# FFN gate and up: hi and lo parts of x as one 512-column moving operand, accumulator halves added afterwards, and new start addresses for TensorE's operands

## The chip, the cores and the metric

One core of a Trainium2 chip runs the whole program. The metric is the device time of one execution in microseconds (us), as a median of several runs. TensorE is called PE in the rows, its weight loads PEld, VectorE DVE, ScalarE ACT, GpSimd POOL, SyncE SP.

## What is computed

A trunk of two layers over 256 tokens of width 1024, all in float32. Cut to what matters here:

```python
D_MODEL = 1024; SEQ = 256; DEPTH = 2; D_FF = 2816

def swiglu(x, wg, wu, wd):
    return (jax.nn.silu(x @ wg) * (x @ wu)) @ wd

for i in range(DEPTH):
    h = h + 0.5 * swiglu(rmsnorm(h, ffn1_norm[i]), ffn1_wg[i], ffn1_wu[i], ffn1_wd[i])
    h = h + hybrid_mixer(rmsnorm(h, mix_norm[i]), ...)
    h = h + 0.5 * swiglu(rmsnorm(h, ffn2_norm[i]), ffn2_wg[i], ffn2_wu[i], ffn2_wd[i])
    gate = jax.nn.sigmoid(rmsnorm(h, ple_norm[i]) @ ple_w_gate[i])
    h = h + gate * (p[i] @ ple_w_proj[i])
return rmsnorm(h, final_norm)
```

So the FFN half-step stands four times in the program: twice in each layer.

## The kernel before

Every large product is done with both operands split into two float32r parts, hi and lo, whose sum is the float32 value. Three products are added in PSUM: hi with hi, hi with lo, lo with hi. Weights come from HBM in chunks of 1 MB, each loaded as two halves (`raw`, five slots) on SP's queue. Each half is split by `split` (lines 97 and 98): ACT copies `raw` to `whi`, DVE subtracts to get `wlo`. `whi` and `wlo` have seven slots each (`NHALF`), so that three and a half chunks are live: the half that is split when half n gives its slot back is half n + 7.

The activations of a stage are turned to [feature, token] and split into `xhi` and `xlo`, eight blocks of 128 features by 256 tokens (`xpair`). Products come in two forms. In `ws` the weights are stationary and 256 columns of x move; `ws2` does two blocks of 128 features into the two halves of one PSUM bank. In `as_` a 128 by 128 block of activations is stationary and up to 512 columns of weights move. All are emitted through `mm` (line 77), so that they share a line; the operands tell them apart, as (moving, stationary).

An FFN stage has 22 chunks of gate and up weights (128 gate features beside 128 up features). The first three go through `up_head`, per token tile and with the activations stationary. The other 19 go through `up(j)`: `ws2` over eight k blocks (48 matmuls of 256 columns) and then `evac(j)`: ACT's Silu of the gate half (line 344), DVE's product with the up half (line 346), and the split into `hh[j]` and `hl[j]`. Then `down` multiplies with `hh` and `hl` stationary, 512 columns of weights moving, for 11 chunks. The stationary activations elsewhere are `xhi`, `xlo` (among others in `Narrow`, the w_o and w_pg projections), `yh`, `yl` (the mixer's second output projection) and `ph`, `pl` (the embedding).

At a stage's seam, `closing`, `prepare` and `turn` run the norm of one token tile under the products of the other. At the very end `Last` (lines 917 to 933) multiplies h by the gain into `xn`, scales it and stores it, tile 0 first. The order on each engine is set by a scheduler of the tile framework from this program order; queues are followed in order.

In the program as built, where an operand begins in its partition, modulo 512 bytes, is: 160 for `whi`, `wlo`, `xhi` and `xlo`; 32 for `hh`, `hl`, `ph` and `pl`; 352 for `yh` and `yl`.

Of the kernel before, what the change touches and what calls it, by code (L numbers as in the profile page):

```python
# [17 lines left out]
NT = 2  # L18
# [17 lines left out]
W2 = NT * HEADS  # L36
ORDER = ("bc8 sc0.0 xs0 sc0.1 bc10 sc0.2 xs1 sc1.0 sc1.1 sc1.2 xs2 xs3 z1.0 sc2.0 sc2.1 z1.1 sc2.2 xs4 bc9 bc11 xs5 "
# [19 lines left out]
def trunk(ctx: ExitStack, tc: tile.TileContext, a: dict, out: bass.AP):  # L57
# [11 lines left out]
    def nm(s):  # L69
        cnt[0] += 1  # L70
        return f"{s}_{cnt[0]}"

    def bank():
        return psp.tile([P, 512], F32, tag="ps", name=nm("ps"))
# [4 lines left out]
    # ---- constants  # L79
# [7 lines left out]
    mhalf = cst.tile([P, 1], F32, name="mhalf")  # L87
    nc.vector.memset(mhalf, -0.5)

    # ---- weights: loaded once each, split into two float32r parts that add up to the float32  # L90
# [14 lines left out]
    def half(raw, kn):  # L105
        """Half a chunk: kn row blocks of 128 as a list of (hi, lo), each [128, CH / 2 / kn]"""
        hi = wp.tile([P, CH // 2], F32R, tag="whi", name=nm("whi"), bufs=NHALF)
        lo = wp.tile([P, CH // 2], F32R, tag="wlo", name=nm("wlo"), bufs=NHALF)
        split(hi, lo, raw)
        hv, lv = (w.rearrange("p (k c) -> p k c", k=kn) for w in (hi, lo))  # L110
        return [(hv[:, k], lv[:, k]) for k in range(kn)]

    # The program is a list of items, emitted in order at the end: (function, keys of the weight chunks it
    # reads). The loads and splits of later chunks are emitted as soon as earlier items have freed their slots.
# [5 lines left out]
    def chunk(name, i, c, kn):  # L120
        """Registers a chunk of weights of kn row blocks; its key"""
        key = (name, i, c)
        sources[key] = (a[name][i, c], kn)
        return key
# [46 lines left out]
    def xpair():  # L171
        hi = act.tile([P, KD, NT, P], F32R, tag="xhi", name=nm("xhi"), bufs=2)
        lo = act.tile([P, KD, NT, P], F32R, tag="xlo", name=nm("xlo"), bufs=2)
        return hi, lo
# [8 lines left out]
    # small products, let in one by one between the large ones  # L183
# [6 lines left out]
    # ---- out[feature, token] for 128-feature blocks: the weights are stationary  # L190
    def ws(o, wc, cols, x, t=None):
        xh, xl = x
        for k in range(KD):
            wh, wl = wc[k]
            rh = xh[:, k] if t is None else xh[:, k, t]
            rl = xl[:, k] if t is None else xl[:, k, t]
            mm(o, wh[:, cols], rh, k == 0, False)
            mm(o, wh[:, cols], rl, False, False)
            mm(o, wl[:, cols], rh, False, k == KD - 1)
            drip()  # L200

    def ws2(ps, wc, x, t=None):
        """Two 128-feature blocks into one bank, for one token tile or both"""
        for b in range(2):
            o = ps[:, b * 256:(b + 1) * 256] if t is None else ps[:, b * 256 + t * P:b * 256 + (t + 1) * P]
            ws(o, wc, slice(b * P, (b + 1) * P), x, t)

    # ---- out[token, feature]: the activations are stationary
    def as_(os, lh, ll, rh, rl, first, last):
        """os: {column block: bank}"""  # L210
        for j, o in os.items():
            sl = slice(j * o.shape[-1], (j + 1) * o.shape[-1])
            mm(o, lh, rh[:, sl], first, False)
            mm(o, lh, rl[:, sl], False, False)
        for j, o in os.items():
            sl = slice(j * o.shape[-1], (j + 1) * o.shape[-1])
            mm(o, ll, rh[:, sl], False, last)
        drip(2)
# [5 lines left out]
    def banks_of(t, sls):  # L224
        """A token tile's accumulators, by the first of their columns"""
        return {(t, sl.start): bank()[:, 0:sl.stop - sl.start] for sl in sls}
# [4 lines left out]
    # ---- [token, feature] -> [feature, token], split  # L231
# [13 lines left out]
    def rstd(parts, scale):  # L245
        v = sm.tile([P, 1], F32, tag="var", name=nm("var"))
        if len(parts) > 1:
            nc.vector.tensor_scalar(v, parts[0], parts[1], EPS, op0=ALU.add, op1=ALU.add)
            for p in parts[2:]:
                nc.vector.tensor_tensor(v, v, p, op=ALU.add)  # L250
        else:
            nc.vector.tensor_scalar(v, parts[0], scale, EPS, op0=ALU.mult, op1=ALU.add)
        r = sm.tile([P, 1], F32, tag="rstd", name=nm("rstd"))
        nc.gpsimd.tensor_tensor(r, v, mhalf, op=ALU.pow)  # L254
        return r

    class Norm:
        """The stage's input from h, per token tile: square(t, sl) the squares of columns sl, prepare(t) the rest of the norm,
        turn(t) to [feature, token]"""
# [25 lines left out]
    # ---- a stage's end and the next one's start, the first token tile ahead of the second: each tile's  # L285
    # elementwise chain runs under the other's products
    def closing(t, steps, finish, prep):
        """The last products of a token tile, one half of the columns after the other"""
        def f(*wcs):
            with ExitStack() as order:  # L290
                if t == 1 and getattr(prep, "first", False):
                    for ins in prep.turned:
                        order.enter_context(tc.issue_after(ins))
                for sl in prep.pieces[t]:
                    for (fn, _), wc in zip(steps, wcs):
                        fn(wc, [sl])
                    finish(t, sl)
                    prep.square(t, sl)
                prep.prepare(t)
        add(f, *[k for _, keys in steps for k in keys])  # L300
# [32 lines left out]
    # ---- feed-forward half-step  # L333
    class FFN:
        def __init__(self, i, gu, dn, gname, ple=None):
# [4 lines left out]

            def evac(j):
                ps = banks.pop(j)
                sg = fp.tile([P, 256], F32, tag="sg", name=nm("sg"), bufs=3)
                nc.scalar.activation(sg, ps[:, 0:256], AF.Silu)
                pr = fp.tile([P, 256], F32, tag="pr", name=nm("pr"), bufs=3)
                nc.vector.tensor_tensor(pr, sg, ps[:, 256:512], op=ALU.mult)  # L346
                hh[j] = fp.tile([P, 256], F32R, tag=f"hh{j}", name=nm("hh"))
                hl[j] = fp.tile([P, 256], F32R, tag=f"hl{j}", name=nm("hl"))
                split(hh[j], hl[j], pr)

            def up(j):
                def f(wc):
                    banks[j] = bank()
                    ws2(banks[j], wc, prep.x)
                    evac(j)
                return f, [chunk(gu, i, j, KD)]

            def up_head(j, t):
                def f(wc):
                    if t == 0:  # L360
                        banks[j] = bank()
                    xh, xl = prep.x
# [50 lines left out]
    # ---- [tokens, K] @ [K, 1024] from four chunks, the first token tile ahead at both ends  # L413
    class Narrow:
        def __init__(self, name, i, x, pieces=(HALVES, HALVES)):
            self.acc = acc = {}

            def run(c, t):
                def f(wc, sls=pieces[t]):
                    if (t, 0) not in acc:  # L420
                        acc.update(banks_of(t, pieces[t]))
                    for k in range(2):
                        kk = c * 2 + k
                        xh, xl = x()
# [6 lines left out]
    # ---- gated per-layer embedding  # L431
    class Ple:
# [16 lines left out]
        def early(self, pool):  # L449
            """Ahead of the stage, in the pool of the one before"""  # L450
# [17 lines left out]
    # ---- token mixing  # L468
    class Mixer:
        def __init__(self, i):  # L470
# [13 lines left out]
            # B and C first: chunks 8..11 of the convolved channels  # L484
# [52 lines left out]
            def z_run(g, kh, ts):  # L537
                def f(wc):
                    xh, xl = S.prep.x
# [15 lines left out]
            # [tokens, K] @ [K, 512]: a half of a projection to D, from two chunks  # L555
# [48 lines left out]
            # the large products in ORDER; the small work by how many of them it comes after its group's last  # L604
            # inner channels
# [34 lines left out]
            # gates and output projections  # L640
# [32 lines left out]
        # the mixer's inner seam, from m_w_out to w_o  # L673
# [42 lines left out]
        def conv_silu(self, ps, blk, dst):  # L716
            """dst [P, 2, 256] = silu(conv(ps) + b) for channel blocks blk, blk + 1"""
# [29 lines left out]
        # time steps: the columns of both parts of the weights are side by side, and added after the transposes;  # L747
        # softplus(x) = max(x, 0) + log1p(e), e = exp(-|x|); log1p(e) = 2 atanh(e / (2 + e))
        def dt_raw(self):
            xh, xl = self.prep.x  # L750
# [7 lines left out]
        def steps(self):  # L758
# [16 lines left out]
            negA = mp.tile([P, HEADS], F32, tag="negA", name=nm("negA"))  # L775
# [20 lines left out]
        # cumulative sums within a chunk, in both layouts, and the first chunk's total  # L796
        def sums(self):
# [11 lines left out]
            self.w0 = w0 = mp.tile([P, HEADS], F32, tag="w0", name=nm("w0"))  # L809
# [10 lines left out]
        # state-space branch, one group of heads: C B^T under the decays  # L820
# [87 lines left out]
    # ---- the whole trunk  # L908
# [5 lines left out]
    class Last(Norm):  # L914
        """The final norm in place of a next stage's input"""
# [5 lines left out]
        def square(self, t, sl):  # L921
            super().square(t, sl)
            if sl.start == 0:
                self.xn[t] = act.tile([P, D], F32, tag=("xhi", "xlo")[t], name=nm("xn"), bufs=2)
# [13 lines left out]
    class First:  # L938
        """The load of x in place of a stage before"""
# [100 lines left out]
```

## Time and profile before

| what | value |
|---|---|
| time, median of 3 runs | 1550.38 us (1548.4 to 1552.99) |
| span of the profiled execution | 1549.5 us |
| PE busy, share of the span | 1529.4 us, 99% |
| weight loads busy | 1396.5 us, 90% |
| DVE busy | 990.3 us, 64% |
| ACT busy | 826.7 us, 53% |
| DMA | 286.38 MB, mean 185 GB/s |

The profiled execution has no time listed beside its span; the span lies between the lowest and the median time of the three runs, 0.9 us under the median. Busy times of PE count each matmul with its modelled end, so neighbours overlap: what a matmul costs in a dense stream is the distance from its start to the next one's start.

### The profile page before, as it was taken

What the parts mean: (1) busy time and instruction counts of PE and PEld (TensorE: products, weight loads), DVE (VectorE), ACT (ScalarE), POOL (GpSimd) and SP (SyncE); (2) the same over time, 40 slices, a digit from 0 to 9 for tenths busy, and PEclk for the clock granted to TensorE, in tenths of its full rate; (3) what the DMA queues carried; (4) which work ended last, traced back from release to release, by engine and by line L of the source; (5) the groups of instructions that cost most, each with busy time, mean ns of one, the idle gap of its engine ahead of it and who ended that gap; (6) DMA issues with size and microseconds to landing.
All of it is one profiled execution on the core that took longest, in us unless ns stands there. A gap on an engine that the chain in (4) does not pass through costs nothing.

```text
span 1549.5 us, 25054 instructions
## 1 busy us (share of the span) xinstructions
PE 1529.4 (99%) x10072; PEld 1396.5 (90%) x10072; DVE 990.3 (64%) x1398; ACT 826.7 (53%) x1110; POOL 25.3 (2%) x41
## 2 busy tenths in 40 slices
PE   7999999999999999999999999999999999999998
PEld 7999889999988889998899988899999887999886
DVE  5555467898865565554675554688979655755545
ACT  5554365667564355543655444675666544544444
POOL 0000000000000000000000000000000000000000
PEclk9999999999999999999999999999999999999999
DMA  7556565555646656666566654665555565665552
GB/s 282 183 188 187 187 189 186 189 186 183 197 150 192 192 186 188 187 187 187 163 201 188 186 183 151 223 198 183 192 176 180 167 191 177 206 189 181 186 152 94
DMA packets 81493, 286.38 MB, mean 185 GB/s; under 512 B 10592, under 2 KB 10976, under 8 KB 81376
## 3 DMA queue, kind: packets, MB, share of 16 engines
q1 hardware_dynamic: 74016, 268.47, 55.0%
q10 hardware_dynamic: 7360, 16.31, 3.2%
q8 instruction: 79, 1.29, 0.3%
q14 instruction: 38, 0.31, 0.1%
HBM read 283.62 MB, written 1.11 MB: 184 GB/s over the span
## 4 chain that ended last, share of the span: by engine, by line
PE 96%; DVE 2%; DMA 1%; ACT 0%; issue 0%; POOL 0%; SPq 0%; POOLq 0%; ACTq 0%; DVEq 0%
PE ps L77 94%; PE ps L238 2%; DVE wlo L98 1%; DMA raw<-in_gu 1%; PE ps L509 0%; ACT whi L97 0%; DVE xn L279 0%; POOL rstd L254 0%; DVE sg L462 0%; PE ps L377 0%; DVE h L463 0%; DVE xlo L242 0%; ACT junk L272 0%; ACT sg L461 0%; DVE h L407 0%
## 5 line engine op out<-in xcount | busy, mean ns | idle before, releaser
L98 DVE TENSOR_TENSOR wlo<-raw,whi 128x1024 fp32r<-128x1024 f32 x508 | 616.7, 1223 | 412.7 <-ACT whi L97 408.4
L97 ACT ACTIVATE whi<-raw 128x1024 fp32r<-128x1024 f32 x508 | 534.2, 1058 | 460.1 <-PE ps L77 430.4
L77 PE MATMUL ps<-xhi,whi 128*128 128x256 f32 x1984 | 571.0, 288 | 0.0
L77 PE MATMUL ps<-xhi,wlo 128*128 128x256 f32 x1984 | 561.4, 283 | 0.0
L77 PE MATMUL ps<-xlo,whi 128*128 128x256 f32 x1984 | 561.3, 283 | 0.0
L77 PEld LDWEIGHTS ps<-xhi,whi 128*128 128x128 f32 x1984 | 380.7, 192 | 2.6 <-issue 1.9
L77 PEld LDWEIGHTS ps<-xlo,whi 128*128 128x128 f32 x1984 | 380.8, 192 | 2.5 <-issue 2.4
L77 PEld LDWEIGHTS ps<-xhi,wlo 128*128 128x128 f32 x1984 | 380.5, 192 | 0.0
L77 PE MATMUL ps<-whi,xhi 128*128 128x512 f32 (+1 forms) x648 | 234.9, 364 | 0.4 <-ACT whi L97 0.2
L77 PE MATMUL ps<-wlo,xhi 128*128 128x512 f32 (+1 forms) x648 | 231.8, 358 | 1.2 <-DVE wlo L98 1.2
L77 PE MATMUL ps<-whi,xlo 128*128 128x512 f32 (+1 forms) x648 | 223.9, 357 | 0.6 <-DVE xlo L242 0.6
L77 PEld LDWEIGHTS ps<-wlo,xhi 128*128 128x128 f32 x648 | 123.4, 190 | 19.4 <-DVE wlo L98 3.1
L77 PEld LDWEIGHTS ps<-whi,xlo 128*128 128x128 f32 x648 | 123.0, 190 | 18.5 <-DVE xlo L242 1.1
L77 PEld LDWEIGHTS ps<-whi,xhi 128*128 128x128 f32 x648 | 123.3, 191 | 17.9 <-ACT whi L97 1.1
L77 PE MATMUL ps<-whi,hh 128*128 128x512 f32 x352 | 139.3, 396 | 0.0
L77 PE MATMUL ps<-wlo,hh 128*128 128x512 f32 x352 | 138.9, 394 | 0.0
L77 PE MATMUL ps<-whi,hl 128*128 128x512 f32 x352 | 115.5, 394 | 0.0
L97 ACT ACTIVATE hh<-pr 128x256 fp32r<-128x256 f32 x76 | 31.8, 418 | 99.5 <-DVE pr L346 99.5
L77 PEld LDWEIGHTS ps<-whi,hl 128*128 128x128 f32 x352 | 66.3, 188 | 15.4
L77 PEld LDWEIGHTS ps<-wlo,hh 128*128 128x128 f32 x352 | 66.4, 188 | 15.2
L77 PEld LDWEIGHTS ps<-whi,hh 128*128 128x128 f32 x352 | 66.4, 188 | 15.1
L724 DVE SCALAR_TENSOR_TENSOR ac<-ps,convw,ac 128x255 f32<-128x255 f32 (+1 forms) x144 | 67.8, 477 | 9.5 <-ACT ac L722 8.2
(149 smaller groups left out, 1120.2 us busy)
## 6 DMA issues: line engine op xcount, KB each, us to landing
raw<-in_gu SPq DMA_DIRECT2D x176, 512.0 KB, 4.3
raw<-in_dn SPq DMA_DIRECT2D x88, 512.0 KB, 4.2
raw<-in_w_xbc SPq DMA_DIRECT2D x48, 512.0 KB, 4.4
raw<-in_w_sc SPq DMA_DIRECT2D x48, 512.0 KB, 4.0
raw<-in_w_z SPq DMA_DIRECT2D x32, 512.0 KB, 3.9
raw<-in_w_mo SPq DMA_DIRECT2D x32, 512.0 KB, 3.8
raw<-in_w_ga SPq DMA_DIRECT2D x16, 512.0 KB, 4.4
m<-acD ACTq DMA_DIRECT2D x16, 512.0 KB, 5.0
```

The source lines that it names most:

```text
L77: nc.tensor.matmul(o, lhsT=l, rhs=r, start=start, stop=stop)
L97: nc.scalar.activation(hi, src, AF.Copy)
L98: nc.vector.tensor_tensor(lo, src, hi.bitcast(F32), op=ALU.subtract)
L238: nc.tensor.transpose(tp[:, j * P:(j + 1) * P], src[:, c:c + P], ident)
L724: nc.vector.scalar_tensor_tensor(ac[:, b, s:256], src[:, 0:256 - s], self.convw[:, q, 3 - s:4 - s], ac[:, b, s:256], op0=ALU.mult, op1=ALU ...
```

## The change

`xpair` becomes one tile `xx` that holds, for each k, the 256 columns of hi and then the 256 columns of lo. For `up(j)`, `wide_ws` takes the place of `ws2`: for each k, `whi` is stationary once and all 512 columns move into a whole bank, and `wlo` is stationary once with the 256 hi columns, added into the bank's first half. Gate and up thus have a bank each, and its second half (hi weights with lo x) is still to be added: `both_parts` lets ACT copy the second half to SBUF and DVE add the first half to it. Silu and the product then work from SBUF. In `Last`, both `xn` tiles are now taken from the tag `xx` (before, one from `xhi` and one from `xlo`). Some small tiles are made larger or share a tag; in the program as built all of `xx`, `whi`, `wlo`, `hh`, `hl`, `ph`, `pl`, `yh` and `yl` then begin at 160 modulo 512 bytes. The other operands of matmuls that move: `xd` from 480 and 224 to 96 and 352, `m` and `btok` from 352 to 32, `bc`, `st` and `xw` from 480 to 96. Other uses of `ws` and `as_` keep their products.

```diff
+LEAD = 8
-    mhalf = cst.tile([P, 1], F32, name="mhalf")
+    mhalf = cst.tile([P, LEAD], F32, name="mhalf")[:, 0:1]
...
     def xpair():
-        hi = act.tile([P, KD, NT, P], F32R, tag="xhi", name=nm("xhi"), bufs=2)
-        lo = act.tile([P, KD, NT, P], F32R, tag="xlo", name=nm("xlo"), bufs=2)
-        return hi, lo
+        both = act.tile([P, KD, 2, NT, P], F32R, tag="xx", name=nm("xx"), bufs=2)
+        return both[:, :, 0], both[:, :, 1], both.rearrange("p k s t c -> p k (s t c)")
...
+    def wide_ws(o, wc, cols, x):
+        xh, _, both = x
+        for k in range(KD):
+            wh, wl = wc[k]
+            if k < KD - 1:
+                mm(o, wh[:, cols], both[:, k], k == 0, False)
+                mm(o[:, 0:256], wl[:, cols], xh[:, k], False, False)
+            else:
+                mm(o[:, 0:256], wl[:, cols], xh[:, k], False, False)
+                mm(o, wh[:, cols], both[:, k], False, True)
...
-        v = sm.tile([P, 1], F32, tag="var", name=nm("var"))
+        v = sm.tile([P, 16], F32, tag="var", name=nm("var"))[:, 0:1]
...
+            def both_parts(ps, tag):
+                v = fp.tile([P, 256], F32, tag=tag, name=nm(tag), bufs=3)
+                nc.scalar.activation(v, ps[:, 256:512], AF.Copy)
+                nc.vector.tensor_tensor(v, v, ps[:, 0:256], op=ALU.add)
+                return v
+
             def evac(j):
-                ps = banks.pop(j)
-                sg = fp.tile([P, 256], F32, tag="sg", name=nm("sg"), bufs=3)
-                nc.scalar.activation(sg, ps[:, 0:256], AF.Silu)
-                pr = fp.tile([P, 256], F32, tag="pr", name=nm("pr"), bufs=3)
-                nc.vector.tensor_tensor(pr, sg, ps[:, 256:512], op=ALU.mult)
+                gate, pr = both_parts(banks[j][0], "sg"), both_parts(banks[j][1], "pr")
+                del banks[j]
+                nc.scalar.activation(gate, gate, AF.Silu)
+                nc.vector.tensor_tensor(pr, gate, pr, op=ALU.mult)
...
             def up(j):
                 def f(wc):
-                    banks[j] = bank()
-                    ws2(banks[j], wc, prep.x)
+                    banks[j] = [bank(), bank()]
+                    for b in range(2):
+                        wide_ws(banks[j][b], wc, slice(b * P, (b + 1) * P), prep.x)
                     evac(j)
...
-            negA = mp.tile([P, HEADS], F32, tag="negA", name=nm("negA"))
+            negA = mp.tile([P, HEADS + 48], F32, tag="negA", name=nm("negA"))[:, 0:HEADS]
...
-            self.w0 = w0 = mp.tile([P, HEADS], F32, tag="w0", name=nm("w0"))
+            self.w0 = w0 = mp.tile([P, HEADS], F32, tag="sp_q", name=nm("w0"))
...
-                self.xn[t] = act.tile([P, D], F32, tag=("xhi", "xlo")[t], name=nm("xn"), bufs=2)
+                self.xn[t] = act.tile([P, D], F32, tag="xx", name=nm("xn"), bufs=2)
```

Outside `up` and the last rows of the program, the order on every engine is the one of before.

On PE, where one chunk of `up` ends and the next begins, the order of before has three matmuls of 256 columns per k (the last three of one chunk and the first three of the next; names carry the buffer's numbers):

```order
L77 MATMUL ps_91_476<-xhi_2_89,whi_58_336 128x256
L77 MATMUL ps_91_476<-xlo_3_90,whi_58_336 128x256
L77 MATMUL ps_91_476<-xhi_2_89,wlo_59_337 128x256
L77 MATMUL ps_102_545<-xhi_2_89,whi_61_342 128x256
L77 MATMUL ps_102_545<-xlo_3_90,whi_61_342 128x256
L77 MATMUL ps_102_545<-xhi_2_89,wlo_62_343 128x256
```

At the same place the changed program has:

```order
L78 MATMUL ps_92_465<-xx_2_89,whi_57_335 128x512
L78 MATMUL ps_92_465<-xx_2_89,wlo_58_336 128x256 x2
L78 MATMUL ps_92_465<-xx_2_89,whi_57_335 128x512
L78 MATMUL ps_103_522<-xx_2_89,whi_60_341 128x512
L78 MATMUL ps_103_522<-xx_2_89,wlo_61_342 128x256
```

One matmul of 512 columns stands where two of 256 stood; a block ends and the next begins with one of 512.

On ACT, one chunk of `up` in the middle of the first FFN, before (a half of the weights split twice, Silu of the finished chunk, its hi part, and the next chunk's first split):

```order
L97 ACTIVATE whi_262_1570<-raw_261_1568 128x1024
L97 ACTIVATE whi_265_1576<-raw_264_1574 128x1024
L344 ACTIVATE sg_257_1560<-ps_256_1511 128x256
L97 ACTIVATE hh_259_1564<-pr_258_1562 128x256
L97 ACTIVATE whi_273_1639<-raw_272_1637 128x1024
```

In the changed program, and below it DVE's rows of the same chunk:

```order
L357 ACTIVATE sg_261_1310<-ps_259_1276 128x256
L364 ACTIVATE sg_261_1310<-sg_261_1310 128x256
L98 ACTIVATE whi_266_1324<-raw_265_1322 128x1024
L357 ACTIVATE pr_262_1313<-ps_260_1277 128x256
L98 ACTIVATE whi_269_1330<-raw_268_1328 128x1024
L98 ACTIVATE hh_263_1318<-pr_262_1313 128x256
```

```order
L358 TENSOR_TENSOR sg_261_1310<-sg_261_1310,ps_259_1276 128x256
L99 TENSOR_TENSOR wlo_267_1325<-raw_265_1322,whi_266_1324 128x1024
L358 TENSOR_TENSOR pr_262_1313<-pr_262_1313,ps_260_1277 128x256
L365 TENSOR_TENSOR pr_262_1313<-sg_261_1310,pr_262_1313 128x256
L99 TENSOR_TENSOR wlo_270_1331<-raw_268_1328,whi_269_1330 128x1024
L99 TENSOR_TENSOR hl_264_1319<-pr_262_1313,hh_263_1318 128x256
```

The gate's copy, add and Silu now stand ahead of the first split, the up part's copy and add between the two splits: ACT has two more instructions of 256 columns a chunk, DVE two more.

At the program's end, DVE's rows for the second token tile, before, with the semaphores that each waits for (DMAHW names are those of transfers):

```order
L463 TENSOR_TENSOR h1_84<-h1_84,sg_2730_15685 128x512 [waits DVE_49]
L925 TENSOR_TENSOR xn_2733_15692<-h1_84,gain_2714_15601 128x512 [waits DVE_49]
L462 TENSOR_TENSOR sg_2734_15712<-sg_2734_15712,pe_2363_13515 128x256 [waits Activation_49]
L463 TENSOR_TENSOR h1_84<-h1_84,sg_2734_15712 128x256 [waits DVE_49]
L925 TENSOR_TENSOR xn_2733_15692<-h1_84,gain_2714_15601 128x256 [waits DVE_49]
L248 TENSOR_SCALAR var_2740_15746<-ss_2732_15690,ss_2736_15717 128x1 [waits Activation_49]
L462 TENSOR_TENSOR sg_2737_15738<-sg_2737_15738,pe_2363_13515 128x256 [waits Activation_49]
```

and in the changed program:

```order
L483 TENSOR_TENSOR h1_84<-h1_84,sg_2794_14837 128x512 [waits DVE_49]
L482 TENSOR_TENSOR sg_2798_14864<-sg_2798_14864,pe_2409_12877 128x256 [waits Activation_49]
L483 TENSOR_TENSOR h1_84<-h1_84,sg_2798_14864 128x256 [waits DVE_49]
L262 TENSOR_SCALAR var_2804_14898<-ss_2796_14842,ss_2800_14869 128x1 [waits Activation_49]
L945 TENSOR_TENSOR xn_2797_14844<-h1_84,gain_2778_14753 128x512 [waits DMAHW3_49,DMAHW2_49]
L945 TENSOR_TENSOR xn_2797_14844<-h1_84,gain_2778_14753 128x256 [waits DVE_49]
L482 TENSOR_TENSOR sg_2801_14890<-sg_2801_14890,pe_2409_12877 128x256 [waits Activation_49]
```

Tile 1's product with the gain has moved behind `var`, ahead of the last piece's `sg`, and waits for the two transfers that store tile 0, whose place it takes.

## Rows read from the trace of the kernel before

**Rows 1.** The page, parts 1 and 4: busy time by engine; the chain's shares.
```profile
span 1549.5 us, 25054 instructions
PE 1529.4 (99%) x10072; PEld 1396.5 (90%) x10072; DVE 990.3 (64%) x1398; ACT 826.7 (53%) x1110; POOL 25.3 (2%) x41
...
PE 96%; DVE 2%; DMA 1%; ACT 0%; issue 0%; POOL 0%; SPq 0%; POOLq 0%; ACTq 0%; DVEq 0%
```

**Rows 2.** Busy time by stretch: us, PE busy (instructions), clock, DMA share, GB/s.
```profile
45.00:132.00 87.00, 87.00 (x727) 1.00 0.58 183
150.00:195.00 45.00, 45.00 (x196) 1.00 0.60 188
```

**Rows 3.** Timeline of PE in w_pg, x stationary: start, us, instruction.
```profile
756.66 0.39 PE L77 MATMUL ps<-whi,xhi 128*128 128x512 f32 x1
...
758.02 0.39 PE L77 MATMUL ps<-whi,xhi 128*128 128x512 f32 x1
```

**Rows 4.** Timeline of PE in the mixer's second output projection, y stationary.
```profile
505.79 0.39 PE L77 MATMUL ps<-whi,yh 128*128 128x512 f32 x1
...
507.16 0.39 PE L77 MATMUL ps<-whi,yh 128*128 128x512 f32 x1
```

**Rows 5.** Groups of PE by shape: count, busy us, mean ns, idle before.
```profile
L77 PE MATMUL ps<-whi,hh 128*128 128x512 f32 x352 | 139.3, 396 | 0.0
L77 PE MATMUL ps<-wlo,yh 128*128 128x512 f32 x128 | 50.3, 393 | 0.0
L77 PE MATMUL ps<-whi,ph 128*128 128x512 f32 x16 | 6.3, 395 | 0.0
L77 PE MATMUL ps<-xd,m 128*128 128x64 f32 x256 | 36.0, 259 | 0.0
```

**Rows 6.** Timeline of PE in the last w_pg, where 512 and 256 columns alternate.
```profile
1528.20 0.39 PE L77 MATMUL ps<-whi,xhi 128*128 128x512 f32 x1
...
1529.59 0.40 PE L77 MATMUL ps<-whi,xhi 128*128 128x512 f32 x1
...
1531.01 0.40 PE L77 MATMUL ps<-whi,xhi 128*128 128x512 f32 x1
```

**Rows 7.** Timeline of ACT over one chunk of `up`, to the next.
```profile
101.97 1.06 ACT L97 ACTIVATE whi<-raw 128x1024 fp32r<-128x1024 f32 x1 [1.17 <-PE ps L77]
...
104.42 0.36 ACT L344 ACTIVATE sg<-ps 128x256 f32<-128x256 f32 x1
106.14 0.42 ACT L97 ACTIVATE hh<-pr 128x256 fp32r<-128x256 f32 x1 [1.35 <-DVE pr L346]
107.72 1.06 ACT L97 ACTIVATE whi<-raw 128x1024 fp32r<-128x1024 f32 x1 [1.17 <-PE ps L77]
```

**Rows 8.** Timeline of DVE over one chunk of `up`.
```profile
104.55 1.22 DVE L98 TENSOR_TENSOR wlo<-raw,whi 128x1024 fp32r<-128x1024 f32 x1 [0.27 <-ACT whi L97]
105.69 0.41 DVE L346 TENSOR_TENSOR pr<-sg,ps 128x256 f32<-128x256 f32 x1
106.59 0.42 DVE L98 TENSOR_TENSOR hl<-pr,hh 128x256 fp32r<-128x256 f32 x1 [0.48 <-ACT hh L97]
```

**Rows 9.** Timeline of DVE and SP at the program's end.
```profile
1539.99 6.24 SPq L933 DMA_DIRECT2D out<-xn  x2
1540.59 0.69 DVE L925 TENSOR_TENSOR xn<-h,gain 128x512 f32<-128x512 f32 x1
1542.11 0.42 DVE L925 TENSOR_TENSOR xn<-h,gain 128x256 f32<-128x256 f32 x1
1542.65 0.21 DVE L248 TENSOR_SCALAR var<-ss,ss 128x1 f32<-128x1 f32 x1
1542.96 0.42 DVE L462 TENSOR_TENSOR sg<-sg,pe 128x256 f32<-128x256 f32 x1
```

**Rows 10.** DMA issues: KB each, median us to landing (last stretch; whole span).
```profile
out<-xn SPq DMA_DIRECT2D x2, 256.0 KB, 2.2
raw<-in_gu SPq DMA_DIRECT2D x176, 512.0 KB, 4.3
```

More of the change, by code (lines that the diff above doesn't have):

```diff
@@ L191, in ws @@
     def ws(o, wc, cols, x, t=None):
-        xh, xl = x
+        xh, xl, _ = x
         for k in range(KD):
@@ L361, in f @@
                         banks[j] = bank()
-                    xh, xl = prep.x
+                    xh, xl, _ = prep.x
                     for k in range(KD):
@@ L423, in f @@
                         kk = c * 2 + k
-                        xh, xl = x()
+                        xh, xl, _ = x()
                         as_(blocks(acc, t, sls), xh[:, kk, t], xl[:, kk, t], *wc[k], kk == 0, kk == KD - 1)
@@ L538, in f @@
                 def f(wc):
-                    xh, xl = S.prep.x
+                    xh, xl, _ = S.prep.x
                     for t in ts:
@@ L749, in dt_raw @@
         def dt_raw(self):
-            xh, xl = self.prep.x
+            xh, xl, _ = self.prep.x
             o = bank()[0:2 * HEADS, 0:NT * P]
```

## The prediction

> **What bounds the kernel now.** I read the page's busy times and chain first. PE is busy for 99% of the span, and 96% of the chain that ended last is PE's own work [rows 1]: nothing that another engine does counts unless PE comes to wait for it. A matmul's own duration says little, since neighbours overlap, so I then took distances between starts. In the body of the first FFN, 87 us hold 727 matmuls of 256 columns, two of which began before the stretch: 87.0 / 725 = 120.0 ns each [rows 2]. In w_pg six matmuls of 512 columns take 1.36 us, 226.7 ns each [rows 3]. [...] So 256 more columns cost 106.7 ns, and 120.0 - 106.7 = 13.3 ns of a matmul do not depend on its columns. PE waits for nothing in the FFN body; it is bound by columns plus 13.3 ns for each matmul.
>
> The same 512 columns are dearer elsewhere. In `down`, with `hh` and `hl` stationary, 45 us hold 196, two begun before: 45.0 / 194 = 232.0 ns [rows 2]. With `yh` and `yl` six take 1.37 us, 228.3 ns [rows 4]. The form is that of w_pg (same calls, same sizes, clock 1.00); what differs is where the stationary operand begins: 160 modulo 512 bytes in w_pg, 32 in `down`, 352 with y.
>
> **The change, part by part.** *The wide moving operand.* There are 76 chunks (4 stages of 19), each with 16 products that replace two matmuls of 256 columns by one of 512, next to one of 256 that stays: 1216 replacements. If prices add, each saves 2 x 120.0 - 226.7 = 13.3 ns, 16.2 us in all. Whether they add when sizes alternate is seen only in the last w_pg, where three of 512 and six of 256 columns take turns. By addition they should take 1.400 us; the rows give 1.39 us and then 1.42 us [rows 6]. Spread over the three of 512, that is 3 ns better to 7 ns worse, so a replacement saves between 16.4 and 6.6 ns, 19.9 to 8.0 us. I take the mean of both passes, 1.7 ns worse: 11.6 ns, **14.1 us**. The chunk shrinks from 48 x 120.0 = 5.76 us to 5.57 us.
>
> [...]
>
> *The start addresses.* If the stationary operand's address is what makes `down` dearer, 352 x 3 matmuls there [rows 5] and 16 x 3 with `ph` and `pl` [rows 5] go from 232.0 to 226.7 ns, 1104 x 5.3 ns = 5.9 us, and 128 x 3 with y [rows 5] go from 228.3 to 226.7 ns, 0.6 us: **6.5 us** together. The ends are nothing and 6.5 us; I take all of it, because three addresses give three spacings under one form. Small fp32 products move too (256 matmuls of `xd` with `m` are the most [rows 5]), to offsets that no row has: at 5 ns either way, 1.3 us, taken as nothing.
>
> [...] The rows show different spacings at the three; that the address causes this, no row shows alone.
>
> *Evacuation of the two banks.* It adds two copies on ACT and two adds on DVE per chunk, and Silu and the product change their source. The copy has the price of `sg` from PSUM, 0.36 us, Silu from SBUF at most that of `hh`, 0.42 us [rows 7]; add and product cost 0.41 and 0.42 us [rows 8]. All lie beside PE's 5.57 us, if the two engines keep up. They run in turn, so the chain counts, not the busy time. With ACT's and DVE's new orders it is: gate's add 0.41, Silu 0.42, first split on ACT 1.06 and on DVE 1.22, up part's add 0.41, product 0.42, second split on DVE 1.22, `hl` 0.42: 5.58 us [rows 7, 8]. Handovers cost about 0.03 us (`pr` ends at 106.10, `hh` starts at 106.14 and ends at 106.56, `hl` starts at 106.59 [rows 7, 8]); with five, 5.73 us. Overlap of neighbours on one engine, as where `pr` starts 0.08 us ahead of the split's end [rows 8], is not taken off. So at worst the chain is 0.16 us longer than PE's chunk and falls behind by 19 x 0.16 = 3.0 us in a stage. What covers it: a half that is split when chunk j leaves its slot is half n + 7, used 2.25 chunks or 12.5 us after j's end; less one whole chain, 6.8 us of lead remain. In `down` each chunk has two splits and nothing else, so the lag is worked off. Banks come round after four chunks of two, which is later still. Cost: nothing; without the cover, up to 3.0 us a stage. The transfers ask for 1 MB per 5.57 in place of 5.76 us, 188 GB/s for 183 [rows 2], with five slots and 4.3 us to landing [rows 10].
>
> *The end.* DVE's product of tile 1 with the gain now waits for tile 0's stores. The second store is issued on SP from 1539.99 us and lands 2.2 us later, 1542.2 us [rows 9, 10]. By then `var` is due, at about 1542.3 us now that two rows ahead of it have gone; the products of 512 and 256 columns follow it, 0.69 + 0.42 us [rows 9], to some 1543.6 us, and the last piece's `sg`, queued behind them on DVE, starts then instead of at 1542.96 us [rows 9]. Nothing runs beside it: **+0.6 us**. If the stores landed 1 us later, 1.6 us.
>
> *Seams.* Orders there are unchanged and waits for hi and lo stay apart: nothing; if a seam's first matmul did wait for lo as well, it would be one DVE step, below 0.7 us, at eight seams or so.
>
> Sum: -14.1 - 6.5 + 0.6 = -20.0 us. From the profiled span, 1549.5 us, that is 1529.5 us; the median of the runs shown is 0.9 us above that span, so about **1530 us**.
>
> **Rivals.** *Addresses do nothing* (5.3 ns belong to something else about `hh`): -13.5 us, 1536.9 us. For it: no row shows the address alone as the cause; against it: y's third value. Chance 0.09. [...] *The wide pair pays nothing*: if 512 columns moved from x cost 240 ns after a 256, both forms cost the same; only addresses stay, -5.9 us, 1544.5 us. Rows 6 show at worst 7 ns, so 0.06. *Most of the 13.3 ns stays*: if it hangs on the columns' being split among weight loads, which are busy for 90% of the span [rows 1], and not on the count of matmuls, and a fifth goes, that is 2.8 us in place of 14.1, 1541.7 us; rows 2 and 3, where loads are the same and the fixed part too, speak against it, 0.03. [...] *Neither does what it says*: 1550 to 1551 us, 0.05. *Evacuation becomes the bound*, on the other side: if the chain on ACT and DVE takes 6.4 us a chunk, a stage loses 19 x 0.83 - 6.8 = 9.0 us, four lose 36 us, and the sum is +16 us, 1566 us. It cancels the gain from (20.0 / 4 + 6.8) / 19 = 0.62 us over PE's chunk, at 6.2 us. For it: 5.73 us is already above 5.57; against it: half a microsecond more has no row. Chance 0.05. Mixtures: 0.02.
>
> **How the numbers follow.** My forecast holds 0.70, with its own range of 1525 to 1534 us: the replacement at its better end, 19.9 us, less 6.5 and plus 0.6 gives 1524.6 us, and at its worse end, 8.0 us, 1536.5 us. The range of 1523 to 1543 us takes in the first and the third rival and the small products' 1.3 us and leaves out no more than 2 in 10. Under 0.3% (4.7 us) a measurement here hardly tells a change from none: faster holds the forecast and the first three rivals, 0.88; same 0.06; slower 0.06.
>
> **What would show it.** In `up`: a pair of 512 and 256 columns every 346 to 349 ns, a chunk in 5.55 to 5.6 us, no idle time of PE. In `down` and with y: 226 to 227 ns. At the end: DVE idle until tile 0's stores land, and `sg` of the last piece about 0.6 us later after PE's last matmul. On ACT and DVE: `whi` waiting for PE in each chunk; if they wait only for each other and PE waits for `wlo`, evacuation is the bound. I am wrong if `down` stays at 232 ns, or if the pair takes 355 ns or more.

## The result: faster by about 1%, 4.9 us short of the forecast

The changed kernel takes 1534.9 us (median of four, 1533.91 to 1535.84) beside 1550.31 us before (1548.4 to 1552.99): ratio 0.9903, 95% interval 0.9891 to 0.9914. The profiled execution took 1533.91 us with a span of 1532.2 us, 17.3 us under the span of before.

The page of the changed kernel answers to [rows 1]: span, busy time by engine, and the chain's shares.

```profile
span 1532.2 us, 22979 instructions
PE 1511.8 (99%) x8856; PEld 1329.6 (87%) x8856; DVE 1041.5 (68%) x1550; ACT 882.6 (58%) x1262; POOL 24.7 (2%) x41
...
PE 96%; DVE 2%; issue 1%; DMA 1%; ACT 0%; POOL 0%; SPq 0%; POOLq 0%; ACTq 0%; DVEq 0%
```

PE has 1216 matmuls less and is still 96% of the chain; the evacuation's 152 new instructions on ACT and on DVE lie beside it. Busy time by stretch, as in [rows 2], shows `up` and then `down`:

```profile
45.00:129.00 84.00, 84.00 (x479) 1.00 0.56 187
145.00:195.00 50.00, 50.00 (x222) 1.00 0.54 176
```

With two begun before each stretch, `down` takes 50.0 / 220 = 227.3 ns a matmul, as its count allows (the distances between starts average 226.7); before it was 232.0 [rows 2]. In `up`, 477 matmuls are 238.5 pairs of 512 and 256 columns: 352.2 ns a pair. Before, the three matmuls took 360. The granted clock is 1.00 in these stretches of both kernels, and from 754 to 759 us, in w_pg of before. PE's timeline in `up`, start and length first, shows where the pair is long:

```profile
101.21 0.28 PE L78 MATMUL ps<-xx,wlo 128*128 128x256 f32 x1
101.32 0.40 PE L78 MATMUL ps<-xx,whi 128*128 128x512 f32 x1
101.56 0.28 PE L78 MATMUL ps<-xx,wlo 128*128 128x256 f32 x1
101.67 0.40 PE L78 MATMUL ps<-xx,whi 128*128 128x512 f32 x1
101.92 0.28 PE L78 MATMUL ps<-xx,wlo 128*128 128x256 f32 x1
102.03 0.40 PE L78 MATMUL ps<-xx,whi 128*128 128x512 f32 x1
102.27 0.28 PE L78 MATMUL ps<-xx,wlo 128*128 128x256 f32 x1
```

From one `wlo` to the next are 0.35, 0.36 and 0.35 us. In nanoseconds of the trace a 512 stands 233, 241 or 236 ahead of the next start, a 256 stands 113, 117 or 120: means of 235.0 and 116.9. So the 512 costs 8.3 ns more than the 226.7 of a stream of its kind, the 256 3 ns less. ACT's timeline over one chunk answers to [rows 7]:

```profile
95.60 0.38 ACT L357 ACTIVATE pr<-ps 128x256 f32<-128x256 f32 x1 [0.54 <-PE ps L78]
95.88 1.06 ACT L98 ACTIVATE whi<-raw 128x1024 fp32r<-128x1024 f32 x1
97.14 0.42 ACT L98 ACTIVATE hh<-pr 128x256 fp32r<-128x256 f32 x1 [0.21 <-DVE pr L365]
98.42 0.38 ACT L357 ACTIVATE sg<-ps 128x256 f32<-128x256 f32 x1 [0.85 <-PE ps L78]
99.29 0.42 ACT L364 ACTIVATE sg<-sg 128x256 f32<-128x256 f32 x1 [0.49 <-DVE sg L358]
99.64 1.06 ACT L98 ACTIVATE whi<-raw 128x1024 fp32r<-128x1024 f32 x1
101.24 0.38 ACT L357 ACTIVATE pr<-ps 128x256 f32<-128x256 f32 x1 [0.54 <-PE ps L78]
```

The chunk repeats every 5.64 us, and ACT waits for PE twice in it, 1.39 us: PE is the bound, and evacuation follows. The distances between PE's starts, summed by kind over the whole program, give the account: x moving -9.4 us; `hh`, `hl` -5.9, `ph`, `pl` -0.3 and y -0.9, together -7.1; x stationary and the small products at the seams -1.4, which no step forecast and which lay between -1.8 and +1.0 in other runs with the same seams; the stretch after PE's last matmul +0.4. The first matmul starts 0.1 us later, and with rounding that makes the 17.3 us.

### The profile page after: what moved, and what is told of

It reads as the page before. It is cut to its first block, busy times and chain, and to the rows that moved or that the text cites. A ratio compares the mean times of both kernels' runs of the same rounds, so it can differ in the third digit from the quotient of the medians.

```text
span 1532.2 us, 22979 instructions
## 1 busy us (share of the span) xinstructions
PE 1511.8 (99%) x8856; PEld 1329.6 (87%) x8856; DVE 1041.5 (68%) x1550; ACT 882.6 (58%) x1262; POOL 24.7 (2%) x41
## 4 chain that ended last, share of the span: by engine, by line
PE 96%; DVE 2%; issue 1%; DMA 1%; ACT 0%; POOL 0%; SPq 0%; POOLq 0%; ACTq 0%; DVEq 0%
PE ps L78 93%; PE ps L252 1%; DVE wlo L99 1%; DMA raw<-in_gu 1%; PE ps L529 0%; DVE xn L293 0%; POOL rstd L268 0%; DVE h L427 0%; DVE xx L256 0%; PE ps L397 0%; ACT whi L98 0%; ACT junk L286 0%; DVE sg L482 0%; DVE h L483 0%; DVE var L262 0%
## 5 line engine op out<-in xcount | busy, mean ns | idle before, releaser
L78 PE MATMUL ps<-xx,whi 128*128 128x256 f32 (+1 forms) x2752 | 707.4, 337 | 0.0
L78 PE MATMUL ps<-xx,wlo 128*128 128x256 f32 x1984 | 533.6, 282 | 0.0
L78 PEld LDWEIGHTS ps<-xx,whi 128*128 128x128 f32 x2752 | 458.4, 190 | 46.5 <-issue 4.3
L78 PEld LDWEIGHTS ps<-xx,wlo 128*128 128x128 f32 x1984 | 376.8, 190 | 13.8
L78 PE MATMUL ps<-whi,xx 128*128 128x512 f32 (+1 forms) x1296 | 362.2, 361 | 0.7 <-DVE xx L256 0.6
L78 PEld LDWEIGHTS ps<-whi,xx 128*128 128x128 f32 x1296 | 231.7, 190 | 35.6 <-DVE xx L256 1.4
L78 PE MATMUL ps<-wlo,xx 128*128 128x512 f32 (+1 forms) x648 | 231.5, 358 | 0.6 <-DVE wlo L99 0.6
L78 PEld LDWEIGHTS ps<-wlo,xx 128*128 128x128 f32 x648 | 123.2, 190 | 18.9 <-DVE wlo L99 2.7
L78 PE MATMUL ps<-whi,yh 128*128 128x512 f32 x128 | 50.0, 390 | 0.0
L78 PE MATMUL ps<-wlo,yh 128*128 128x512 f32 x128 | 49.8, 389 | 0.0
```

Of the source, the lines that this page charges most:

```text
L78: nc.tensor.matmul(o, lhsT=l, rhs=r, start=start, stop=stop)
```

## The experiments

Two theories stood at first. One: the wide pair lost 5.6 ns against 346.7 because the sizes take turns, and the address part is the start address alone. The other: 512 columns from `xx` are dearer in themselves, and `down` has its gain from something else in the change.

**The parts alone.** The kernel before with only the paddings (hh, hl, ph, pl, yh, yl at 160):

```diff
+LEAD = 8
...
+    mhalf = cst.tile([P, LEAD], F32, name="mhalf")[:, 0:1]
...
+        v = sm.tile([P, 16], F32, tag="var", name=nm("var"))[:, 0:1]
...
+            negA = mp.tile([P, HEADS + 48], F32, tag="negA", name=nm("negA"))[:, 0:HEADS]
...
+            self.w0 = w0 = mp.tile([P, HEADS], F32, tag="sp_q", name=nm("w0"))
```

> The kernel before with only the paddings of the small tiles: hh, hl, ph, pl, yh and yl begin at 160 modulo 512 bytes, everything else as before. Theory 1 (the start address is the cause): down and y at 226.7 ns, 7.1 us faster, 1543.2 us. Theory 2 (the wide operand or what surrounds it had changed down's spacing): down stays at 232.0 ns, 1550 us.

And the changed kernel without these paddings:

> The changed kernel without the paddings: hh, hl, ph, pl at 32 and yh, yl at 352 modulo 512 bytes, as before. Theory 1 (the two parts add): down back at 232.0 and y at 228.3 ns, 7.1 us slower than the changed kernel, 1542 us, 8.3 us under before. Theory 2 (the parts are not independent): down at 227 ns, 1535 us.

Addresses alone: 1544.11 us (1543.54 to 1544.33) against 1550.79 us, ratio 0.9959 (0.9945 to 0.9972). Wide operand alone: 1542.02 us (1541.09 to 1543.51), ratio 0.9947 (0.9934 to 0.9959). Busy time in `down`, first of the kernel with addresses alone, then of that with the wide operand alone:

```profile
145.00:195.00 50.00, 50.00 (x222) 1.00 0.60 190
```

```profile
145.00:195.00 50.00, 50.00 (x217) 1.00 0.54 178
```

227.3 and 232.6 ns. The address term comes from the start addresses and from nothing else of the change, it is 6.7 us, and the two parts add (6.7 + 8.8 = 15.5 us, and 15.4 for the whole change).

**Sizes in groups.** All wide products of a block first, then all with `wlo` (the same sum in another order):

```diff
-        for k in range(KD):
-            wh, wl = wc[k]
...
+        for k in range(KD - 1):
+            mm(o, wc[k][0][:, cols], both[:, k], k == 0, False)
+        for k in range(KD):
+            mm(o[:, 0:256], wc[k][1][:, cols], xh[:, k], False, False)
+        mm(o, wc[KD - 1][0][:, cols], both[:, KD - 1], False, True)
```

> Per block of 128 features, `up` does the wide products of all k first and the 256-column ones with `wlo` behind them; the sum is the same, in another order. Theory 1 (what the pair lost against 346.7 ns comes from sizes taking turns): the 512-column matmuls from xx fall from 235.0 to 227 ns, a pair takes 347 ns, the chunk 5.55 us, and 1216 x 5.7 ns = 6.9 us go: 1528 us. Theory 2 (512 columns moved from xx are dearer in themselves, with whi stationary): they stay at 235 ns, and the 256-column ones return to 120.0, so that the pair takes 355 ns and the time is 1535 to 1538 us. The two are told apart by the spacing of 512-column matmuls that follow each other.

1531.24 us (1531.16 to 1531.59), ratio 0.9877 (0.9863 to 0.989): 3.7 us under the changed kernel's median, about half of what the first theory asked, and outside of the second's range. PE's timeline now shows whole groups, their number at the end of each line:

```profile
101.02 2.00 PE L78 MATMUL ps<-xx,whi 128*128 128x512 f32 x8
102.86 1.11 PE L78 MATMUL ps<-xx,wlo 128*128 128x256 f32 x8
103.81 0.40 PE L78 MATMUL ps<-xx,whi 128*128 128x512 f32 x1
```

Eight of 512 take 1.84 us, 230.0 ns each, eight of 256 take 0.95 us. In nanoseconds the eight stand 233, 236, 229, 232, 231, 227, 226, 227 apart, and the first two of 256 stand 113 and 119, then 120. So neither theory was whole: here a change from 256 to 512 columns costs some 28 ns over the next five matmuls of 512 (1161 for 5 x 226.7 ns) and gives 8 back at the return (232 for 2 x 120.0 ns). The same five numbers, to a nanosecond, stand in the kernel with addresses alone where `up` ends and `down` begins; its PE timeline there:

```profile
143.26 0.28 PE L78 MATMUL ps<-xhi,wlo 128*128 128x256 f32 x1
143.38 0.40 PE L78 MATMUL ps<-whi,hh 128*128 128x512 f32 x1
143.61 0.40 PE L78 MATMUL ps<-wlo,hh 128*128 128x512 f32 x1
143.85 0.39 PE L78 MATMUL ps<-whi,hh 128*128 128x512 f32 x1
144.08 0.40 PE L78 MATMUL ps<-wlo,hh 128*128 128x512 f32 x1
144.31 0.62 PE L78 MATMUL ps<-whi,hl 128*128 128x512 f32 x2
144.77 0.39 PE L78 MATMUL ps<-whi,hh 128*128 128x512 f32 x1
```

Five matmuls from 143.38 to 144.54 take 233, 236, 228, 233 and 231 ns, and from then on 226 or 227. Neither x nor `xx` moves there. Both blocks of a chunk together test it:

```diff
...
+        for o, cols in blocks_:
+            for k in range(KD - 1):
+                mm(o, wc[k][0][:, cols], both[:, k], k == 0, False)
+        for o, cols in blocks_:
+            for k in range(KD):
+                mm(o[:, 0:256], wc[k][1][:, cols], xh[:, k], False, False)
+        for o, cols in blocks_:
+            mm(o, wc[KD - 1][0][:, cols], both[:, KD - 1], False, True)
```

> As the run with blocks of 8, but both blocks of a chunk together: 16 products of 512 columns, then 16 of 256. In the run with 8, the 512-column ones stood 233, 236, 229, 232, 231, then 227 ns apart. Theory 1 (the first five after a change of size are dearer, whatever their k): the five come once in 16, the other eleven are at 227, and half of the 152 changes go, each worth 27 - 7 = 20 ns: 1.5 us less than with blocks of 8, about 1529.7 us. Theory 2 (the spacing hangs on k, that is, on the place in xx): the series of eight comes twice in the sixteen, and the time stays at 1531.2 us.

```profile
99.64 3.82 PE L78 MATMUL ps<-xx,whi 128*128 128x512 f32 x16
103.29 2.08 PE L78 MATMUL ps<-xx,wlo 128*128 128x256 f32 x16
105.20 0.40 PE L78 MATMUL ps<-xx,whi 128*128 128x512 f32 x1
```

Sixteen take 3.65 us, 228.1 ns each; the five dear ones come once, then eleven at 226 or 227. The place of k in `xx` has no part in it. The time, 1530.56 us (1529.18 to 1533.48), is too wide to tell from groups of eight; the sum of x moving does: -9.4 us in turns, -13.0 in groups of 8, -14.5 in groups of 16. By the account of 28 - 8 = 20 ns a round it would be 16.2 - 152 x 0.020 = 13.2 and 16.2 - 76 x 0.020 = 14.7 us.

**Which address is a good one.** First all offsets of `hh` and `hl`, in steps of 32 bytes:

```diff
-                hl[j] = fp.tile([P, 256], F32R, tag=f"hl{j}", name=nm("hl"))
+                hl[j] = fp.tile([P, 264], F32R, tag=f"hl{j}", name=nm("hl"))[:, 0:256]
...
```

> The changed kernel with hl tiles 32 bytes longer, so that block j of hh and hl begins at 160 + 32 j modulo 512 bytes: all 16 offsets in down, each with 48 to 96 matmuls. Theory 1 (the spacing depends on the stationary start address alone): a map with 226.7 at 160, 228.3 at 352 and 232.0 at 32, in between unknown; mean somewhere at 227 to 232 ns, so the time is 1535 to 1541 us. Theory 2 (what counts is the distance to the moving operand's address, also 160): the map is lowest at 160 and rises with the distance on both sides. Theory 3 (no cause in the address): one value at all offsets.

1539.67 us in a single execution. Blocks take their places in the order in which their tiles are made (3, 0, 1, 2, 4 and on), so block 3 is the one at 160. Each offset keeps for only six matmuls before another follows. At 416 they stand 227, 226, 227, 227, 226, 235 apart (the last before the next offset), at 160 233, 231, 226, 227, 227, 228, at 192 232, 235, 231, 235, 232, 236, and offsets 256 bytes apart have much the same series (256 and 0 both 231, 231, 238, 237 within). Only 160 and 416 settle. Since six are hardly more than the five that follow a change, the next kernel keeps one offset for a whole stage, by a tile of 64, 128, 192 or 256 bytes at the head of the stage's pool:

```diff
+            shift = (64, 128, 192, 256)[2 * i + (gname == "ffn2_norm")] // 4
+            self.shift = lambda: nc.vector.memset(fp.tile([P, shift], F32, tag="shift", name=nm("shift")), 0.0)
...
+            self.shift()
```

> The changed kernel with hh and hl at one start address per FFN stage: 224, 288, 352 and 416 modulo 512 bytes in turn, moving operand at 160 as before. In the map of all offsets only 160 and 416 settled, and each offset read like the one 256 bytes away, but its runs had six matmuls. Theory 1 (only the stationary start modulo 256 counts, and one of eight places is good): 416 at 226.7, 288 at 232.4 (as 32), 352 at 229, 224 at 231 to 235 ns; about 264 x (6 + 6 + 2) = 4 us slower than the changed kernel. Theory 2 (the map's runs of six showed changes of address, not addresses): all four stages settle at 226.7 ns, 1535 us.

Busy time in the four `down`, at 224, 288, 352 and 416:

```profile
145.00:195.00 50.00, 50.00 (x216) 1.00 0.54 177
685.00:735.00 50.00, 50.00 (x217) 1.00 0.55 172
905.00:955.00 50.00, 50.00 (x220) 1.00 0.53 174
1443.00:1493.00 50.00, 50.00 (x222) 1.00 0.56 179
```

Counts fall from 220 to 214 without the two begun before; by the distances between starts it is 233.3, 232.4, 228.9 and 226.7 ns. So it is the address, it repeats after 256 bytes in these runs (288 gives 232.4 ns where 32 gave 232.0, and 416 gives 226.7 like 160), and the time of a single execution, 1537.61 us, is 2.7 us over the changed kernel's median (in spans 1535.9 against 1532.2 us). Whether the place itself counts or its distance from the other operand, moving both tells:

```diff
-LEAD = 8
+LEAD = 24
```

> The changed kernel with everything behind one small tile 64 bytes further: both operands of the large products at 224 modulo 512 bytes. Theory 1 (the distance of the two operands modulo 256 bytes counts, and it stays 0): down at 226.7 ns, 1535 us. Theory 2 (the place itself counts, 160 modulo 256 being the good one): down and all other products of 512 columns at 231 to 235 ns, over 2800 x 5 ns = 14 us slower, 1549 us or more.

1535.68 us (1533.69 to 1536.98), ratio 0.9903 (0.9883 to 0.9923). Busy time in `down`, both operands at 224:

```profile
145.00:195.00 50.00, 50.00 (x222) 1.00 0.56 180
```

226.7 ns by the distances between starts (227.3 by the count), where 224 beside 160 gave 233.3. What counts in these runs is the distance: stationary start less moving start, modulo 256.

**The same distance for 256 columns.** The kernel before, with 64 bytes ahead of the activations:

```diff
+    nc.vector.memset(act.tile([P, 16], F32, tag="apart", name="apart"), 0.0)
     h = [act.tile([P, D], F32, tag=f"h{t}", name=f"h{t}") for t in range(NT)]
```

> The kernel before with 64 bytes put ahead of the activations alone: x at 224 modulo 512 bytes, weights still at 160, hh, hl, ph, pl at 96, yh, yl at 416. The map of distances (stationary start less moving start, modulo 256: 0 gives 226.7 ns, 64 gives 233.3, 128 gives 232.4, 192 gives 228.9) then forecasts for 512 columns: x stationary, distance 64, 1320 x 6.6 = 8.7 us slower; hh and its like, distance 192, 1104 x 3.5 = 3.9 us faster; y, distance 0, 0.8 us faster; 4.0 us slower together. Theory 1 (256 columns do not feel the distance, their 120.0 ns have another cause): up stays at 120.0 ns, 1554.4 us. Theory 2 (they feel it as those of 512 do: weights stationary, x moving is distance 192, 2.2 ns): 5952 x 2.2 = 13 us more, 1567 us. Theory 3 (the map is not one of distances): the forecasts for hh and y fail.

1533.29 us (1530.76 to 1533.4) against 1550.05 us, ratio 0.9888 (0.9871 to 0.9904). Theories 1 and 2 both fell: 256 columns feel the distance, but with the other sign. Busy time in `up` and in `down`:

```profile
45.00:132.00 87.00, 87.00 (x741) 1.00 0.60 183
145.00:195.00 50.00, 50.00 (x220) 1.00 0.56 178
```

`up` takes 87.0 / 739 = 117.7 ns a matmul, where it took 120.0 [rows 2]. By the distances between starts, matmuls of 256 columns stand 117.2 apart on average at distance 192 (x moving) and 115.1 at distance 64 (x stationary), against 120.0 at 0 in both forms: what is dear for 512 columns (228.9 ns at 192 and 233.3 at 64, against 226.7 at 0) is cheap for 256. But the two averages are mixtures of the same two levels. Busy time in two stretches at distance 64 and one at 192:

```profile
20.00:32.00 12.00, 12.00 (x104) 1.00 0.83 293
560.00:568.00 8.00, 8.00 (x73) 1.00 0.28 89
235.00:250.00 15.00, 15.00 (x135) 1.00 0.63 181
```

By the distances between starts they run at 117.8, 113.3 and 113.3 ns, and `up` above at 117.8. In the second FFN, `up` itself goes at 113.3 ns until the transposes below, and at 117.8 from 577 us to its end:

```profile
575.79 0.82 PE L378 MATMUL ps<-ident,pr 128*128 128x128 f32 x6
```

So what the runs show for 256 columns is two levels off distance 0, 113.3 and 117.8 ns, at 64 as at 192. The 87 us of `up` above are at 117.8 on average, and in the second FFN the level changes over an interruption by transposes; what picks the level stays open. For 512 the map held, and theory 3 fell: 233.3 ns at distance 64 (233.3 forecast), 228.9 at 192 (228.9), 226.8 at 0 (226.7). The sums: x moving -15.9 us, `hh` and its like -3.8, y -0.8, x stationary +3.2; the first matmul starts 0.7 us earlier. One line gives 16.8 us, about as much as the whole change.

**Evacuation made longer.** Extra copies in place in the chunk's chains, which leave the values as they are: one pair (up part), two pairs (both parts), four pairs:

```diff
+                nc.scalar.activation(pr, pr, AF.Copy)
+                nc.vector.tensor_copy(pr, pr)
```

> The changed kernel with one more copy on ACT and one on DVE, in place, in the up part's chain of each chunk (values unchanged): 0.87 us more. Theory 1 (the prediction's arithmetic: ACT and DVE run in turn, 5.73 us a chunk, lead of 6.8 us a stage): 6.6 us a chunk against PE's 5.64, a stage loses 19 x 0.96 - 6.8 = 11.4 us, 46 us in all, 1581 us. Theory 2 (the two engines overlap more than that, since ACT waits for PE 1.4 us in each chunk): the chunk stays at 5.64 us on PE, 1535 us.

> The changed kernel with one more copy on ACT and one on DVE, in place, in both the gate's and the up part's chain (values unchanged): 1.7 us more a chunk if all is in turn. Theory 1 (chain in turn, the prediction's 5.73 us): 7.4 us a chunk, a stage loses 19 x 1.8 - 6.8 = 27 us, 109 us in all, 1644 us. Theory 2 (the parts' chains overlap, and what counts is the busier engine, about 4.6 us of ACT and 4.7 us of DVE a chunk): the chunk stays at 5.64 us on PE, 1535 us.

> As with one more copy on each engine in both chains, but two more in each: 3.4 us more a chunk if all is in turn. Theory 1 (chain in turn): 9.1 us a chunk, over 1700 us. Theory 2 (the busier engine counts): ACT 5.4 and DVE 5.3 us a chunk against PE's 5.64, just hidden, 1535 to 1545 us. In between, a chunk of 6 to 7 us on ACT would be 19 x 1 - 6.8 = 12 us a stage and more, 1580 us and up.

1535.57 us (1535.19 to 1535.95; ratio 0.9905, 0.9891 to 0.992), and in single executions 1535.54 and 1532.72 us. ACT's timeline with four pairs:

```profile
97.72 0.39 ACT L357 ACTIVATE sg<-ps 128x256 f32<-128x256 f32 x1 [0.67 <-PE ps L78]
98.00 0.41 ACT L365 ACTIVATE pr<-pr 128x256 f32<-128x256 f32 x1
98.59 0.42 ACT L367 ACTIVATE sg<-sg 128x256 f32<-128x256 f32 x1 [0.18 <-DVE sg L358]
98.95 1.06 ACT L98 ACTIVATE whi<-raw 128x1024 fp32r<-128x1024 f32 x1
...
103.36 0.39 ACT L357 ACTIVATE sg<-ps 128x256 f32<-128x256 f32 x1 [0.67 <-PE ps L78]
```

The chunk is 5.64 us as ever, and ACT still waits 0.67 us for PE and 0.18 us for DVE: `pr` of one part is copied between steps of the other's `sg`. A copy takes 0.41 us on ACT and, by DVE's timeline, less than the 0.41 that the expectations took:

```profile
96.21 0.29 DVE L370 COPY sg<-sg 128x256 f32<-128x256 f32 x1
```

The arithmetic in turn is out: 4 x (0.41 + 0.29) = 2.8 us more of chain found room beside PE, and ACT's own work is still 5.64 - 0.85 = 4.8 us a chunk. Where evacuation would become the bound, none of these reached.

**The end.** Groups of 16, and one `xx` tile for both `xn`:

```diff
-                self.xn[t] = act.tile([P, D], F32, tag="xx", name=nm("xn"), bufs=2)
+                if t == 0:
+                    self.place = act.tile([P, NT, D], F32, tag="xx", name=nm("xn"), bufs=2)
+                self.xn[t] = self.place[:, t]
```

> Groups of 16 as in the run before, and at the end both xn tiles share one xx tile, so that tile 1's product with the gain needs no place that tile 0's stores give back. Theory 1 (the moved products, 1.02 us ahead of the last piece's sg, lengthen the end): they stand ahead of var again, and from PE's last matmul to sg it takes 0.73 us as before the change, in place of 1.10: 0.4 us less than groups of 16 alone, about 1529.5 to 1530.2 us. Theory 2 (the end is set by something else, such as the store's landing): 1.10 us stays.

1529.37 us (1529.0 to 1529.94), ratio 0.9871 (0.9855 to 0.9888): the lowest median of all. The times alone do not tell it from groups of 16 without the shared tile; the rows do. DVE's timeline at the end answers to [rows 9], first of the changed kernel, whose last matmul starts at 1524.51 us, then of this one, where it starts at 1519.95:

```profile
1524.55 0.21 DVE L262 TENSOR_SCALAR var<-ss,ss 128x1 f32<-128x1 f32 x1 [0.58 <-ACT junk L286]
1524.68 1.02 DVE L945 TENSOR_TENSOR xn<-h,gain 128x512 f32<-128x512 f32 x2
1525.61 0.42 DVE L482 TENSOR_TENSOR sg<-sg,pe 128x256 f32<-128x256 f32 x1
```

```profile
1519.84 0.42 DVE L947 TENSOR_TENSOR xn<-h,gain 128x256 f32<-128x256 f32 x1
1520.38 0.21 DVE L263 TENSOR_SCALAR var<-ss,ss 128x1 f32<-128x1 f32 x1
1520.69 0.43 DVE L482 TENSOR_TENSOR sg<-sg,pe 128x256 f32<-128x256 f32 x1
```

From the last matmul to the last piece's `sg` it takes 1.10 us in the changed kernel and 0.74 here (0.73 before, whose last matmul starts at 1542.23). The moved products are what cost 0.4 us.

## Why the prediction was right, and where it was off

**The bound.** Right: PE's spacing sets the time before and after. But the step "13.3 ns of a matmul do not depend on its columns" was too general. It comes from two spacings at distance 0, 120.0 ns for 256 columns and 226.7 for 512, whose difference is 106.7. Against this 106.7 and twice it, 213.3, an estimate from these two alone, 256 columns leave 6.6 or 11.1 ns off distance 0 (the levels 113.3 and 117.8), and 512 columns leave 15.6 at distance 192 (228.9) and 20.0 at 64 (233.3). That both operands of `up` and w_pg began at 160 made it look like a constant.

**The wide operand.** The mis-sized term: 9.4 us measured for 14.1 taken. That a matmul less for each replacement saves time is shown by groups of 16, which give 14.5 us, 11.9 ns for each of 1216. What failed is "I take the mean of both passes, 1.7 ns worse" [rows 6]: with sizes in turns all along, a pair is 5.6 ns worse than by addition, near the second pass's 7 (in nanoseconds of the trace that pass takes 1415 for 1400, 5.0 for each matmul of 512). The first pass came out of a long stream of 512 columns, and `up` never does. The row to go by was the second pass. In spans the forecast missed by 20.0 - 17.3 = 2.7 us: 4.7 here, less 0.6 at the addresses, 0.2 at the end and 1.4 at the seams, and 0.2 of the first matmul's start and rounding. The 1.4 us at the seams is luck, since they go either way from run to run. The medians' 4.9 us hold 1.8 more, since the median lies 2.7 us over the profiled span and not 0.9 as before, and 0.4 of rounding 1530.4 to 1530.

**The addresses.** Right in cause and size: 7.1 us in the trace for 6.5, and 6.7 us by themselves. The rival that they do nothing fell with the kernel that had them alone: 32, 160 and 352 bytes are not alike (232.0, 226.7 and 228.3 ns before). What the prediction did not see is that it is a distance between two operands. With clock, sizes and order alike, the spacing of 512 columns was 226.7 to 233.3 ns by nothing but the distance of the two starts. Why the distance counts, no run shows.

**Evacuation.** Right that it costs nothing, wrong why: it was not the 6.8 us of lead that covered a chain of 5.73 us. A chain 2.8 us longer in turn cost nothing either, so the rival's turning point, 6.2 us, was no such point.

**The end.** Right in mechanism: 0.4 us for 0.6. The products run behind `var` and ahead of `sg`; the later of tile 0's two stores, issued at 1522.26 us, landed by 1524.51, and the first product starts at 1524.68, so no wait came on top.

**The other rivals.** "The wide pair pays nothing" (355 ns or more) fell at 352.2; with the pair in groups it pays nearly all. "Most of the 13.3 ns stays" fell by the same runs. "Neither does what it says" fell with either part alone.

## What to carry to other kernels

Before an operation is rebuilt to save a fixed cost per matmul, move its operands: read the start addresses modulo 256 bytes and try other distances, since here 64 bytes of padding gave 16.8 us, more than the wide operand alone (8.8), and the good distance differs here by the number of columns: 0 for 512 (226.7 ns), 64 or 192 for 256 (113.3 or 117.8 against 120.0). If matmuls of two sizes share a stream, put equal ones in runs as long as banks allow (here 9.4 us saved in turns, 14.5 in groups of 16), and price a new mix by a row that stands in the same mix, not by one at the end of a long even run. A chain over two engines that runs once a chunk is not priced by its length in turn where its parts can overlap: here 2.8 us more in turn left the chunk at 5.64 us.

Open are three things. The kernel before with weights at distance 64 over x (in place of 192) was not tried: by these rows x stationary with 512 columns would be at 228.9 in place of 233.3 ns, 1320 x 4.4 = 6 us less than the 1533 us of x apart, an estimate of some 1527 us. What `ws` would do there cannot be said, since 256 columns show both levels at either distance. What holds a stream of 256 columns at 113.3 and not 117.8 ns is the second. And whether the pair of 512 and 256 has a better distance than 0 is not known, since every run of it had both at the same address modulo 256.

## What was not expected of the hardware

In these runs the spacing of matmuls depends on the distance of stationary and moving start addresses modulo 256 bytes, and in opposite ways: 512 columns 226.7, 233.3, 232.4 and 228.9 ns at 0, 64, 128 and 192; 256 columns 120.0 at 0, and 113.3 or 117.8 at both 64 and 192. After a change from 256 to 512 columns at distance 0, five matmuls stand 233, 236, 229, 232 and 231 ns apart before 226.7 is reached, and two of 256 behind 512 are 7 and 1 ns short.
